# An encoder block on one core: the MLP's weight preparation as two streams, and earlier operands for its second product

## Chip, cores and metric

The kernel runs on one core of one Trainium2 chip. The metric is the device time of one execution in microseconds (us). Engines are named as the profile names them: PE (TensorE), DVE (VectorE), ACT (ScalarE), POOL (GpSimd) and SP, whose queue issues the DMAs.

## What is computed

A hybrid encoder block over 1024 tokens of 1024 channels, in float32. Only its last line matters here:

```
h = rms_norm(x, norm2_g) @ w_mlp_in            # 1024x1024 by 1024x4096
x = x + square(relu(h)) @ w_mlp_out            # 1024x4096 by 4096x1024
```

## The kernel before

**Precision.** Each float32 matrix is scaled by a power of two and split into two float16 parts, hi on ACT (a scaled copy) and lo on DVE (the scaled value less hi, one SCALAR_TENSOR_TENSOR). A product is three passes over these parts (PASSES, L473). The power of two comes from a bound on the matrix: ACT squares it and sums along each row, DVE adds the row sums (`sum_of`, L933) and copies the result to a bfloat16 column, PE sums over the 128 partitions with a matmul against ones (`all_sum`, L197; a 128x1 result, "ones" in the profile), and DVE makes the scale of it (`scale_of`, L940). `scale_of` holds the ones matmul back until PE has been given n whole units of work since the sum.

**Strassen's scheme in Winograd's form.** Both MLP products are done with seven half-size products instead of eight, so sums of quarters of each matrix are needed: for weights POOL makes them (`forms_sum`, L1067, four additions), for activations `sums` (L1274).

**First product.** The 4096 hidden channels are 16 groups (chunks) q of 128 + 128. A group is seven units (`seven`, L1126; `quad`, L1578), each 12 matmuls into one PSUM bank; the eight banks go round, so that a unit's bank is free again only when the unit eight places before it (sums over partitions counted) has been read. DVE combines each bank with earlier ones into `as`. Groups 0 and 1 are done in two halves of 256 tokens, 0, 1, 0, 1, because the last tokens' activations come late. When a group is done, `h_done` (L1551) gives its result relu and square on ACT, the four sums for the second product on POOL (for q of 0 and 1 on DVE), and stores it to HBM (`hs`).

**Weight preparation of a group** has two halves. `sums1(q)` (L1354): when the two raw tiles of weights are loaded, eight scalings in place on ACT (`rows_scaled`, L949), two squares with row sums on ACT (`squares`, L959), four sums on POOL, then `sum_of`. `prep1(q)` (L1369): `scale_of`, then, once group q - 3 is done on PE (`gate`, L1340) and its tile is free, the split `forms_split` (L1095) in four steps, each a hi part and a lo part (`parts`, L1081). After the second lo part two raw tiles count as free, and `load_upto` (L231) issues the loads of the next two; there are five raw tiles (`rawp`, L77). In the kernel before, one stream does split(q), then sums(q + 1), then split(q + 1) and so on.

**Second product.** 28 operand pairs, seven to each of four stages, are made by `prep2` (L1648), each an activation form and a weight form with hi and lo parts (`ops`), and taken by 4 units each (L1780). For stage 0 `first2` (L1730) issues the loads of w_2 (`w2x`) and of the first stored form.

**What orders the work.** Everything is emitted by one Python program; each engine gets its instructions in the order of emission, and waits for other engines through semaphores at its head. After each unit `unit` (L204) emits the unit's reading of its bank, delayed by one unit (`late`), then alternates `step` (advance every generator in `fg`: `h_done` and the like) and `tick` (advance the first generator of `bg`: preparation). A generator that yields WAIT lets the next one in `bg` run, if `side[0]` is set. In the first product a unit has 2 steps and 5 ticks (3 steps in groups 0 and 1's halves), in the second 2 and 4.

Of the kernel before, what the change touches and what calls it, by code (L numbers as in the profile page):

```python
# [10 lines left out]
F32 = mybir.dt.float32  # L11
F16 = mybir.dt.float16
# [58 lines left out]
def encoder_block(ctx: ExitStack, tc: tile.TileContext, x, weights, cols, gqk, rel, masks, out):  # L71
# [102 lines left out]
        forced[0] = False  # L174

    late, units, forced, side, splitting = [], [0], [False], [False], [False]
    work = [0]

    def apart(mark, n=3, of=units):
        while of[0] < mark + n and not forced[0]:  # L180
            yield WAIT
# [22 lines left out]
    def unit(mms, post=None, steps=0, ticks=0):  # L204

        for ps, l, r, a, b in mms:
            T.matmul(ps, l, r, start=a, stop=b)  # L207
        units[0] += 1
        work[0] += len(mms) * mms[0][0].shape[-1]
        settle()  # L210
        if post:
            late.append(post)
        for i in range(max(steps, ticks)):
            if i < steps:
                step()
            if i < ticks:
                tick()

    def settle():
# [861 lines left out]
    def parts(todo, s, then):  # L1081

        prev = None
        for n, it in enumerate(todo + [None]):
            if prev:
                o, w = prev
                V.scalar_tensor_tensor(o(1), w, sc[:, s], o(0), op0=OP.mult, op1=OP.subtract)
                then(n - 1)
            if it:
                o, w = it  # L1090
                A.activation(o(0), w, AF.Copy, scale=sc[:, s])
            prev = it
            yield
# [245 lines left out]

    def gate(i):  # L1340
        while pe_done[0] < i - 2:
            yield

    def need(i):
        while i not in ready:
# [23 lines left out]
    def prep1(q):  # L1369

        ch = c1[q]
        s, ch.inv = yield from scale_of(ch.sum, 9, 1)
        yield from gate(q)
        pool, tag = TAGS[q % 3]
        P = P1[q] = pool.tile([128, 7 if q else 8, 2, 512], F16, name="w16_1", tag=tag)
        yield from forms_split(ch, tsum[q], s, P)
        ready.add(q)
        if 1 < q < 15:
            yield from sums1(q + 1)

    SQJ = U2[1][:, 0, :, :, 384:512].rearrange("p s k t -> p (s k) t").bitcast(BF16)
    scaled = []
# [143 lines left out]
    def last_pair():  # L1526
        sq(7, 1)()
        normal(7, row3(7))
        yield from wait(3)
        form_sums()  # L1530
        high(3, 0), high(3, 1)
        yield from wait(6)
        low(3, 0)
        yield from wait(3)
        bg.append(sums1(2))
        bg.extend(prep1(q) for q in range(2, 16))
        yield from wait(6)
        low(3, 1)
        limit[0] = 10 ** 6
        load_upto(done[0] + 5)  # L1540
# [10 lines left out]
    def h_done(q, c0=0, c1=512, wait1=0, wait2=0):  # L1551

        f = AS[q] if c1 < 512 else AS.pop(q)
        v = f[:, :, c0:c1]
        yield from wait(wait1)
        A.activation(v[:, 0:4], v[:, 0:4], AF.Relu)
        yield
        A.activation(v[:, 0:4], v[:, 0:4], AF.Square, scale=sc[:, c1w[q].inv],
                     accum_out=sc[:, at(bsum[q // 4], 4 if c1 < 512 else q % 4)])
        yield  # L1560
        yield from wait(wait2)
        if q > 1:
            yield from sums(v, G)
        else:
            for _ in sums(v, V):
                pass
        if c1 < 512:
            return
        SP.dma_start(HS[q // 4][:, :, q % 4], f)
        live.remove(q)  # L1570
        if q % 4 == 3:
            m = tmp()
            V.tensor_reduce(sc[:, m], sc[:, bsum[q // 4]], axis=AX, op=OP.max)
            yield
            yield from pow2(m, 14, *R[q // 4])
            r_ready[q // 4] = True

    def quad(q, c0=0, c1=512):  # L1578
        need(q)
        if c0 == 0:  # L1580
            while q - 2 in live:
                step()
            live.add(q)
            AS[q] = w4p.tile([128, 7, 512], F32, name="as", tag="as")
        ps = {}
        z = [AS[q][:, i, c0:c1] for i in range(7)]
        if q == 2:
            z[4:6] = extra

        def post6(ps):  # L1590
            V.tensor_tensor(z[5], ps[6], z[4], op=OP.add)
            if c0:
                post5(ps)

        def post5(ps):
            V.tensor_tensor(z[1], ps[5], z[5], op=OP.subtract)

        def post7(ps):
            V.tensor_tensor(z[6], ps[7], z[5], op=OP.add)
            V.tensor_tensor(z[2], ps[4], z[6], op=OP.add)  # L1600
            V.tensor_tensor(z[3], ps[5], z[6], op=OP.subtract)

        def post3(ps):
            V.tensor_tensor(z[1], ps[3], z[1], op=OP.add)
            if q == 0:
                fg.append(h_done(q, c0, c1, 3, 4 if c0 else 24))
            elif c1 == 512:
                fg.append(h_done(q, 0, c1, *((2, 6) if q == 1 else ())))
        seven(P1[q], actU2, c0, c1, {
            1: lambda ps: A.activation(z[4], ps[1], AF.Copy),  # L1610
            6: post6, 5: None if c0 else post5,
            2: lambda ps: V.tensor_tensor(z[0], ps[2], z[4], op=OP.add),
            7: post7, 3: post3}, 2 if c1 == 512 else 3, 5, (1, 2, 5, 4, 6, 7, 3) if c0 else (1, 6, 5, 4, 2, 7, 3))

    def whole(q):
        quad(q)
        pe_done[0] = q + 1
# [7 lines left out]
    quad(1, 256, 512)  # L1625
    pe_done[0] = 2
    held[0] = 0
    for q in range(2, 14):
        whole(q)


    OPS, X2 = {}, {}
# [15 lines left out]
    def prep2(s):  # L1648
# [23 lines left out]
            G.tensor_tensor(T2[:, i], w12[i], w22[i], op=OP.add)  # L1672
            G.tensor_tensor(T2[:, i], T2[:, i], w11[i], op=OP.add)
        yield
        if s == 0:
            yield from gate(17)
            P = OPS[17] = TAGS[17 % 3][0].tile([128, 2, 2, 2048], F16, name="ops", tag=TAGS[17 % 3][1])
            later["h", 1] = P[:, 0].rearrange("p w m -> p (w m)").bitcast(F32).rearrange("p (k t) -> p k t", k=4)
            SP.dma_start(later["h", 1], HS[0][:, ORDER[1][0]])
        sw, inv = yield from scale_of(sums, 0)  # L1680
        fw = keep()
        mul(iR, sw, fw)
# [2 lines left out]
        for o, (f, name) in enumerate(ORDER):  # L1685
# [1 line left out]
            i = 16 + n  # L1687
            yield from gate(i)
            pool, tag = TAGS[i % 3]
            if n > 1:  # L1690
                OPS[i] = pool.tile([128, 2, 2, 2048], F16, name="ops", tag=tag)
            P = OPS[i]
            while ("h", n) not in later:
                yield
            if 1 < n < 25:
# [2 lines left out]
            A.activation(P[:, 1, 0], hf, AF.Copy, scale=sc[:, Rs])  # L1698
            yield
            V.scalar_tensor_tensor(P[:, 1, 1], hf, sc[:, Rs], P[:, 1, 0], op0=OP.mult, op1=OP.subtract)  # L1700
            w = {"w11": w11, "t1": w11, "t3": w12, "w21": w21, "w22": w22}.get(name) or [T2[:, i] for i in range(2)]
            for i2 in range(2):
                A.activation(P[:, 0, 0, 1024 * i2:1024 * i2 + 1024], w[i2], AF.Copy, scale=sc[:, fw])
            yield
            for i2 in range(2):
                sl = slice(1024 * i2, 1024 * i2 + 1024)
                V.scalar_tensor_tensor(P[:, 0, 1, sl], w[i2], sc[:, fw], P[:, 0, 0, sl], op0=OP.mult, op1=OP.subtract)
                yield
            ready.add(i)
            if name == "w11":  # L1710
# [24 lines left out]
        later["t2"] = lambda: h0[:, 1].rearrange("p (a k) t -> p a (k t)", a=2)  # L1735
        yield from wait(12)

    bg.append(first2())
    bg.append(prep2(0))
    whole(14)  # L1740
    whole(15)


    later["hf"] = base.tile([128, 4, 4, 512], F32, name="hf", tag="U")
# [129 lines left out]
```

## Time and profile before

| | us |
|---|---|
| three runs | 1237.73, 1239.75, 1241.18 |
| median | 1239.75 |
| the profiled execution's own time | 1236.77 |
| its span, first to last instruction | 1235.0 |
| mean granted clock of PE over the span | 0.994 |
| first product, groups 2 to 15, on PE | 680.5 to 938.2 |
| second product on PE | 938.2 to the end |

How to read it: spans and stage bounds are from one profiled execution. In timelines the columns are start, time until the last one ends, engine, line, operation, tile written and tiles read, shapes, count, and in brackets the idle time of the engine before it with what ended it. Most operations of DVE and ACT carry the line of a helper, L66, and are told apart by their tiles: `raw` are raw weights, `tsum` their sums, `w` the float16 parts, `as` the products of a group, `ops` operands of the second product, `hf`, `h` and `hs` the stored forms.

### The profile page before, as it was taken

Reading aid. Unit: us, or ns where it says so; the run is one execution under the profiler, and the core shown is the slowest. Engines: PE = TensorE matmul, PEld = TensorE weight load, DVE = VectorE, ACT = ScalarE, POOL = GpSimd, SP = SyncE. Lnnn points to the kernel's source line nnn. Section 1 sums busy time; section 2 is a strip of 40 time slices with the busy share of each in tenths; the row PEclk is TensorE's granted clock in tenths of the full one; section 3 lists DMA queues with packets and bytes.
Section 4 is the critical chain, followed back from the end, with each engine's and each line's share of the span. In section 5 each row is a group of like instructions: output and inputs, shape, how many; then the busy total and the mean of one; then the engine's idle time right before and its main releaser. Section 6 shows DMA issues by size and latency. Waiting matters only on the chain.

```text
span 1235.0 us, 16691 instructions
## 1 busy us (share of the span) xinstructions
PE 1196.9 (97%) x6102; PEld 576.9 (47%) x6102; DVE 936.9 (76%) x1747; ACT 765.9 (62%) x1185; POOL 430.3 (35%) x289
## 2 busy tenths in 40 slices
PE   5989999999899999999999999999999999999998
PEld 3534445555444444444458444444444444444444
DVE  6668778888558786877878664555547999999997
ACT  6777667768644454535768777777775763646430
POOL 2440003232212111101003466655648373463562
PEclk8999999999899999999999999999999999999999
DMA  6558455565761211216096653454474844435202
GB/s 258 107 200 178 103 118 112 116 153 105 131 154 34 69 52 51 69 35 255 18 174 152 205 170 137 162 187 142 140 290 162 313 155 159 168 116 222 103 35 103
DMA packets 170867, 173.34 MB, mean 140 GB/s; under 512 B 131488, under 2 KB 132000, under 8 KB 166688
## 3 DMA queue, kind: packets, MB, share of 16 engines
q1 hardware_dynamic: 170784, 172.27, 47.2%
q8 instruction: 48, 0.79, 0.3%
q14 instruction: 35, 0.29, 0.1%
HBM read 102.51 MB, written 37.75 MB: 114 GB/s over the span
## 4 chain that ended last, share of the span: by engine, by line
PE 40%; DVE 6%; ACT 2%; issue 2%; DMA 1%; DVEq 0%; ACTq 0%
PE ps_d L207 16%; PE ps_s L207 14%; PE ps_o L207 10%; DVE as L66 1%; DVE ops L66 1%; DVE w L66 1%; DVE form L66 1%; ACT as L66 1%; DVE v L66 1%; DMA u2T<-v 1%; DMA u2x<-v 1%; ACT ops L66 1%; DVE x L66 0%; DVE sc L66 0%; ACT u2x L66 0%
## 5 line engine op out<-in xcount | busy, mean ns | idle before, releaser
L207 PEld LDWEIGHTS <-ops 128*128 128x128 f16 x1356 | 132.4, 98 | 159.9 <-issue 2.7
L207 PEld LDWEIGHTS <-w 128*128 128x128 f16 x1368 | 132.8, 98 | 143.5 <-issue 3.8
L924 PE MATMUL ps_d<-uT,w_ws 128*128 128x512 f16 x576 | 136.7, 382 | 0.0
L207 PE MATMUL ps_s<-ops 128*128 128x512 f16 (+1 forms) x528 | 118.3, 374 | 0.0
L207 PE MATMUL ps_d<-ops 128*128 128x512 f16 x504 | 115.6, 379 | 0.0
L66 ACT ACTIVATE ops<-hf,sc 128x2048 f16<-128x2048 f32 x26 | 52.0, 1999 | 94.0 <-PE ps_d L207 52.7
L207 PE MATMUL ps_d<-u2T,w 128*128 128x512 f16 (+1 forms) x504 | 110.3, 371 | 0.0
L1074 POOL TENSOR_TENSOR tsum<-raw 128x512 f32<-128x512 f32 x28 | 46.6, 1677 | 148.1 <-ACT raw L66 148.1
L207 PEld LDWEIGHTS <-uT 128*128 128x128 f16 x648 | 64.9, 101 | 70.5 <-issue 5.6
L1278 POOL TENSOR_TENSOR as<-as 128x512 f32<-128x512 f32 x56 | 76.7, 1370 | 41.4 <-ACT as L66 38.1
L207 PEld LDWEIGHTS <-w_s 128*128 128x128 f16 x588 | 56.9, 98 | 68.6 <-DVE w_s L66 0.6
L924 PEld LDWEIGHTS <-w_ws 128*128 128x128 f16 x576 | 56.1, 98 | 59.7 <-issue 2.0
L207 PE MATMUL ps_s<-u2x,w 128*128 128x512 f16 (+1 forms) x348 | 78.6, 375 | 0.0
L207 PE MATMUL ps_o<-ops 128*128 128x512 f16 x324 | 74.3, 379 | 2.4 <-DVE as L66 2.4
L66 DVE SCALAR_TENSOR_TENSOR ops<-hf,sc,ops 128x2048 f16<-128x2048 f32 x26 | 71.7, 2759 | 5.7 <-ACT ops L66 5.7
L66 ACT ACTIVATE raw<-raw,sc 128x256 f32<-128x256 f32 x172 | 71.1, 494 | 6.7 <-DMA raw<-in_weights 6.7
L66 DVE TENSOR_TENSOR as<-ps_s,as 128x512 f32<-128x512 f32 (+1 forms) x38 | 23.4, 616 | 58.5 <-ACT as L66 57.9
L66 DVE TENSOR_SCALAR sc<-sc 128x1 int32<-128x1 int32 (+3 forms) x380 | 57.6, 167 | 12.9 <-ACT sq L66 4.3
L1074 POOL TENSOR_TENSOR gsum<-raw 128x512 f32<-128x512 f32 x14 | 18.5, 1340 | 136.8 <-issue 52.3
L66 ACT ACTIVATE w<-raw,sc 128x512 f16<-128x512 f32 (+1 forms) x29 | 25.4, 920 | 50.8 <-DVE sc L66 50.8
L66 ACT ACTIVATE sz<-sz,sc 128x384 f32<-128x384 f32 (+1 forms) x64 | 37.2, 581 | 26.8 <-DVE sc L66 26.6
L66 DVE SCALAR_TENSOR_TENSOR w_ws<-raw,sc,w_ws 128x512 f16<-128x512 f32 (+2 forms) x72 | 48.5, 712 | 6.7 <-ACT w_ws L66 6.7
(261 smaller groups left out, 2548.6 us busy)
## 6 DMA issues: line engine op xcount, KB each, us to landing
raw<-in_weights SPq DMA_DIRECT2D x89, 512.0 KB, 5.5
hs<-as SPq DMA_DIRECT2D x16, 1792.0 KB, 8.7
hf<-hs SPq DMA_DIRECT2D x26, 1024.0 KB, 6.7
w2x<-in_weights SPq DMA_DIRECT2D x16, 512.0 KB, 8.3
raw<-in_weights SPq DMA_DIRECT2D x16, 384.0 KB, 3.7
xt<-in_x SPq DMA_DIRECT2D x8, 512.0 KB, 9.8
gs<-s SPq DMA_DIRECT2D x4, 1024.0 KB, 6.4
x<-in_x SPq DMA_DIRECT2D x8, 512.0 KB, 10.0
```

The costliest lines, as they stand in the source:

```text
L66: return f(out, *a, **kw)
L207: T.matmul(ps, l, r, start=a, stop=b)
L924: T.matmul(ps, l, r, start=a, stop=b)
L1074: G.tensor_tensor(t[:, o], a, b, op=OP.add)
L1278: sub.tensor_tensor(z[o], z[a], z[b], op=op)
```

## The change

Weight preparation becomes two streams in `bg`, both started where the single one was. `all_sums` runs `sums1` for q = 2 to 15 and may be up to three chunks ahead of the split (it waits until q - 3 is ready). `all_preps` runs `prep1` for q = 2 to 15, each waiting until its chunk's sums are done, and then `first2` and `prep2(0)`. With `side[0]` set the splits run when the sums wait and the other way round. `scale_of` holds its ones matmul back by 2 units instead of 1 for q over 2. From group 2 to 15 `pace[0]` is 1: within one unit, ticks stop as soon as one lo part has been issued (`spent`). `first2` and `prep2(0)`, which stood before groups 14 and 15 in the program, now follow the last split; the second operand pair takes its tile and loads its form inside the loop, and then waits for 2 units' work. The four sums of group 1's result go to POOL and no longer wait 6 steps.

```diff
--- before.py
+++ after.py
@@ -174,7 +174,7 @@
         forced[0] = False
 
     late, units, forced, side, splitting = [], [0], [False], [False], [False]
-    work = [0]
+    work, spent, pace = [0], [0], [0]
 
     def apart(mark, n=3, of=units):
         while of[0] < mark + n and not forced[0]:
@@ -210,10 +210,11 @@
         settle()
         if post:
             late.append(post)
+        spent[0] = 0
         for i in range(max(steps, ticks)):
             if i < steps:
                 step()
-            if i < ticks:
+            if i < ticks and (not pace[0] or spent[0] < pace[0]):
                 tick()
 
     def settle():
@@ -1085,6 +1086,7 @@
             if prev:
                 o, w = prev
                 V.scalar_tensor_tensor(o(1), w, sc[:, s], o(0), op0=OP.mult, op1=OP.subtract)
+                spent[0] += 1
                 then(n - 1)
             if it:
                 o, w = it
@@ -1339,7 +1341,7 @@
 
     def gate(i):
         while pe_done[0] < i - 2:
-            yield
+            yield WAIT
 
     def need(i):
         while i not in ready:
@@ -1369,14 +1371,30 @@
     def prep1(q):
 
         ch = c1[q]
-        s, ch.inv = yield from scale_of(ch.sum, 9, 1)
+        while q > 1 and q not in summed:
+            yield WAIT
+        s, ch.inv = yield from scale_of(ch.sum, 9, 2 if q > 2 else 1)
         yield from gate(q)
         pool, tag = TAGS[q % 3]
         P = P1[q] = pool.tile([128, 7 if q else 8, 2, 512], F16, name="w16_1", tag=tag)
         yield from forms_split(ch, tsum[q], s, P)
         ready.add(q)
-        if 1 < q < 15:
-            yield from sums1(q + 1)
+
+    summed = set()
+
+    def all_sums():
+        for q in range(2, 16):
+            while q > 4 and q - 3 not in ready:
+                yield WAIT
+            yield from sums1(q)
+            summed.add(q)
+
+    def all_preps():
+        for q in range(2, 16):
+            yield from prep1(q)
+        side[0] = False
+        yield from first2()
+        yield from prep2(0)
 
     SQJ = U2[1][:, 0, :, :, 384:512].rearrange("p s k t -> p (s k) t").bitcast(BF16)
     scaled = []
@@ -1532,8 +1550,8 @@
         yield from wait(6)
         low(3, 0)
         yield from wait(3)
-        bg.append(sums1(2))
-        bg.extend(prep1(q) for q in range(2, 16))
+        side[0] = True
+        bg.extend([all_sums(), all_preps()])
         yield from wait(6)
         low(3, 1)
         limit[0] = 10 ** 6
@@ -1559,7 +1577,7 @@
                      accum_out=sc[:, at(bsum[q // 4], 4 if c1 < 512 else q % 4)])
         yield
         yield from wait(wait2)
-        if q > 1:
+        if q > 0:
             yield from sums(v, G)
         else:
             for _ in sums(v, V):
@@ -1605,7 +1623,7 @@
             if q == 0:
                 fg.append(h_done(q, c0, c1, 3, 4 if c0 else 24))
             elif c1 == 512:
-                fg.append(h_done(q, 0, c1, *((2, 6) if q == 1 else ())))
+                fg.append(h_done(q, 0, c1, *((2, 0) if q == 1 else ())))
         seven(P1[q], actU2, c0, c1, {
             1: lambda ps: A.activation(z[4], ps[1], AF.Copy),
             6: post6, 5: None if c0 else post5,
@@ -1625,8 +1643,6 @@
     quad(1, 256, 512)
     pe_done[0] = 2
     held[0] = 0
-    for q in range(2, 14):
-        whole(q)
 
 
     OPS, X2 = {}, {}
@@ -1672,11 +1688,6 @@
             G.tensor_tensor(T2[:, i], w12[i], w22[i], op=OP.add)
             G.tensor_tensor(T2[:, i], T2[:, i], w11[i], op=OP.add)
         yield
-        if s == 0:
-            yield from gate(17)
-            P = OPS[17] = TAGS[17 % 3][0].tile([128, 2, 2, 2048], F16, name="ops", tag=TAGS[17 % 3][1])
-            later["h", 1] = P[:, 0].rearrange("p w m -> p (w m)").bitcast(F32).rearrange("p (k t) -> p k t", k=4)
-            SP.dma_start(later["h", 1], HS[0][:, ORDER[1][0]])
         sw, inv = yield from scale_of(sums, 0)
         fw = keep()
         mul(iR, sw, fw)
@@ -1687,9 +1698,13 @@
             i = 16 + n
             yield from gate(i)
             pool, tag = TAGS[i % 3]
-            if n > 1:
+            if n:
                 OPS[i] = pool.tile([128, 2, 2, 2048], F16, name="ops", tag=tag)
             P = OPS[i]
+            if n == 1:
+                later["h", 1] = P[:, 0].rearrange("p w m -> p (w m)").bitcast(F32).rearrange("p (k t) -> p k t", k=4)
+                SP.dma_start(later["h", 1], HS[0][:, ORDER[1][0]])
+                yield from apart(work[0], 2 * 6144, work)
             while ("h", n) not in later:
                 yield
             if 1 < n < 25:
@@ -1698,6 +1713,7 @@
             A.activation(P[:, 1, 0], hf, AF.Copy, scale=sc[:, Rs])
             yield
             V.scalar_tensor_tensor(P[:, 1, 1], hf, sc[:, Rs], P[:, 1, 0], op0=OP.mult, op1=OP.subtract)
+            spent[0] += 1
             w = {"w11": w11, "t1": w11, "t3": w12, "w21": w21, "w22": w22}.get(name) or [T2[:, i] for i in range(2)]
             for i2 in range(2):
                 A.activation(P[:, 0, 0, 1024 * i2:1024 * i2 + 1024], w[i2], AF.Copy, scale=sc[:, fw])
@@ -1705,6 +1721,7 @@
             for i2 in range(2):
                 sl = slice(1024 * i2, 1024 * i2 + 1024)
                 V.scalar_tensor_tensor(P[:, 0, 1, sl], w[i2], sc[:, fw], P[:, 0, 0, sl], op0=OP.mult, op1=OP.subtract)
+                spent[0] += 1
                 yield
             ready.add(i)
             if name == "w11":
@@ -1735,10 +1752,10 @@
         later["t2"] = lambda: h0[:, 1].rearrange("p (a k) t -> p a (k t)", a=2)
         yield from wait(12)
 
-    bg.append(first2())
-    bg.append(prep2(0))
-    whole(14)
-    whole(15)
+    pace[0] = 1
+    for q in range(2, 16):
+        whole(q)
+    pace[0] = 0
 
 
     later["hf"] = base.tile([128, 4, 4, 512], F32, name="hf", tag="U")
```

## Prediction

> **What bounds the kernel now.** I read the page's first lines, then the stage's row in the table of windows, then who kept PE waiting from 680 us on.
>
> ```profile
> span 1235.0 us, 16691 instructions
> ...
> PE 1196.9 (97%) x6102; PEld 576.9 (47%) x6102; DVE 936.9 (76%) x1747; ACT 765.9 (62%) x1185; POOL 430.3 (35%) x289
> ```
>
> ```profile
> 680.00:902.00 222.00, 218.80 (x1028) 99.42 (x1026) 127.11 (x253) 163.65 (x241) 128.25 (x92) 1.00 0.50 166
> ```
>
> ```profile
> PE ps_o L207 <- DVE as L66: 4.8, 2, 2.4
> PE ps_s L198 <- DVE ones L66: 0.8, 1, 0.8
> ```
>
> PE is the bound. In the first MLP product it computes 218.80 of 222 us at granted clock 1.00; ACT works 163.65, DVE 127.11, POOL 128.25. From 680 us to the end PE waits 4.8 + 0.8 = 5.6 us in all. That is everything the change can win there, 0.45% of 1235.0; the rest can only be lost.
>
> The units around it, by their starts on PE:
>
> ```profile
> 671.34 1.47 PE L207 MATMUL ps_d<-u2T,w 128*128 128x256 f16 x12
> 672.65 1.47 PE L207 MATMUL ps_s<-u2T,raw 128*128 128x256 f16 x12
> ...
> 680.54 2.75 PE L207 MATMUL ps_d<-u2T,w 128*128 128x512 f16 x12
> ...
> 698.69 2.75 PE L207 MATMUL ps_d<-u2T,w 128*128 128x512 f16 x12
> ...
> 870.78 2.75 PE L207 MATMUL ps_o<-u2T,w 128*128 128x512 f16 x12
> ...
> 948.51 2.75 PE L207 MATMUL ps_o<-ops 128*128 128x512 f16 x12 [2.38 <-DVE as L66]
> ```
>
> A half unit takes 1.31 us (672.65 - 671.34), a whole one twice that, 2.59, so a group of seven whole units 18.15. Group 2 starts at 680.54, group 3 at 698.69. Group 3 holds the first 2.4 and the 0.8; the last unit of the first operand pair of the second product holds the other 2.4. The unit at 870.78 is the third of group 12.
>
> **The change, part by part.** Nothing is added to the arithmetic: the same lo parts, scalings and loads are issued in another order (only group 1's four sums go from DVE to POOL). So the cost is what now stands ahead of what. I went through the order in which each engine gets its instructions in the changed kernel and gave each the time of its row here.
>
> *Start-up, groups 0 and 1.* The sums of chunk 3 (eight scalings of raw weights and two squares on ACT) now stand ahead of the split of chunk 2; before, they stood behind it.
>
> ```profile
> 662.67 1.76 ACT L66 ACTIVATE w<-raw,sc 128x512 f16<-128x512 f32 x2 [1.32 <-DVE sc L66]
> ...
> 666.41 0.36 ACT L66 ACTIVATE as<-ps_s 128x256 f32<-128x256 f32 x1
> 667.94 3.30 ACT L66 ACTIVATE raw<-raw,sc 128x256 f32<-128x256 f32 x8 [1.17 <-DMA raw<-in_weights]
> 671.15 1.04 ACT L66 ACTIVATE tsum<-raw 128x1024 f32<-128x1024 f32 x1
> ...
> 673.37 0.36 ACT L66 ACTIVATE as<-ps_d 128x256 f32<-128x256 f32 x1
> ```
>
> ```profile
> 663.57 2.90 SPq L229 DMA_DIRECT2D raw<-in_weights  x4
> ```
>
> The raw weights land at 667.94 whatever ACT does: their load is issued only at 663.57, behind the transposes, and this the change leaves alone. So ACT now idles until 667.94, scales and squares until 673.4, and only then does the split (666.41 - 662.67 = 3.74 us), until 677.1, and the copy of a bank (0.36) until 677.5. On DVE, in order:
>
> ```profile
> 734.15 1.94 DVE L66 SCALAR_TENSOR_TENSOR w<-raw,sc,w 128x512 f16<-128x512 f32 x2
> 736.00 2.48 DVE L66 SCALAR_TENSOR_TENSOR w<-tsum,sc,w 128x1024 f16<-128x1024 f32 x2
> 738.39 0.68 DVE L66 TENSOR_TENSOR as<-ps_s,as 128x512 f32<-128x512 f32 x1
> ...
> 739.72 1.28 DVE L66 TENSOR_TENSOR as<-ps_o,as 128x512 f32<-128x512 f32 x2
> ...
> 746.51 0.16 DVE L66 CAST ones<-sc 128x1 bf16<-128x1 f32 x1
> ...
> 749.31 0.78 DVE L66 TENSOR_SCALAR sc<-sc 128x1 int32<-128x1 int32 x5
> ```
>
> Four lo parts trail the four hi parts; from the first hi (674.1) they take 1.85 + 2.4, to 678.5; then one combination (half width, 0.4) and a reduce and the cast (0.16 each and the gap) for the sum over partitions of the next chunk (0.35), to 679.3. That sum's matmul on PE stands right before the unit that started at 672.65 and waits for the cast: **6.7 us** of idle PE. Four in-place sums (half width, 1.8) and one combination later the second unit after it gets its bank, 0.8 late; and in group 2 the next sum's matmul waits likewise for chunk 3's split, which ACT ends at about 690.6 and DVE at 692.3, 1.6 after PE is there. Together 9.1 us: group 2 starts at 688.1, group 3 at 707.8.
>
> *The loop of groups 3 to 11.* Here lies the larger term. In each group the changed order on ACT is: relu, first hi part, square, second and third hi part, **four scalings of a raw tile whose load was issued only when this group's first lo part freed its buffer**, two squares, and then the fourth hi part. Behind that one's lo part stand on DVE all combinations of this group's last four units, and behind the last of them the next group's relu. That is a circle. "Sums ahead" is ahead of the split, but five raw tiles do not let the loads be ahead. Its prices, from a steady group of before:
>
> ```profile
> 777.38 1.89 ACT L66 ACTIVATE as<-as 128x2048 f32<-128x2048 f32 x1
> ...
> 779.30 2.00 ACT L66 ACTIVATE as<-as,sc 128x2048 f32<-128x2048 f32 x1
> ...
> 786.37 1.76 ACT L66 ACTIVATE w<-raw,sc 128x512 f16<-128x512 f32 x2 [4.49 <-DVE sc L66]
> 788.04 2.17 ACT L66 ACTIVATE w<-tsum,sc 128x1024 f16<-128x1024 f32 x2
> ```
>
> ```profile
> raw<-in_weights SPq DMA_DIRECT2D x6, 512.0 KB, 3.9
> ```
>
> ```profile
> hs<-as SPq DMA_DIRECT2D x8, 1792.0 KB, 8.7
> raw<-in_weights SPq DMA_DIRECT2D x14, 512.0 KB, 6.9
> ```
>
> ```profile
> L66 DVE SCALAR_TENSOR_TENSOR w<-tsum,sc,w x24: 1272/1279/2289, 700.0 to 900.6; 128x1024 f16<-128x1024 f32 x24
> ```
>
> Relu 1.92 (779.30 - 777.38), first hi 0.7, lo 0.75, load 4.0 (3.9 is the median from 450 to 500 us, where a raw load runs alone; 6.9 that from 740 to 880 us, where it is issued beside the 1792 KB store; in the new order the store is nearly through) = 7.4. ACT's own queue gets there at 1.92 + 0.6 + 2.0 + 1.07 + 0.5 + 1.04 = 7.1, so the load ends last. Scalings 1.6 (half of 3.2), squares 2.2, hi 1.1: 12.3. Lo part: 1.28 alone, 2.29 where POOL adds beside it. Then five combinations (two starts 1.33 apart, 0.67 each with the last's end: 3.3), reduce and cast 0.35, six small operations 1.0: 4.65. Sum: **18.25 or 19.25 us** against PE's 18.15. In the new order POOL starts this chunk's sums just before that lo part, as it does here at
>
> ```profile
> 699.98 4.49 DVE L66 SCALAR_TENSOR_TENSOR w<-tsum,sc,w 128x1024 f16<-128x1024 f32 x2
> ```
>
> ```profile
> 701.47 4.13 POOL L1074 TENSOR_TENSOR tsum<-tsum,raw 128x512 f32<-128x512 f32 x2 [0.28 <-ACT tsum L66]
> ```
>
> where two lo parts took 4.49, so I take 19.25; 18.25 stays as the lower end. The Trainium skill, "GPSIMD Engine Reference", section 1, Specifications, says that GpSimd's SBUF interfaces are shared with VectorE and that instructions with two SBUF inputs contend; by that rule, which speaks against this change, the lo part (two SBUF inputs) is slow in every group and the dear end holds. The row's minimum and median, 1272 and 1279, do not yet show it; its maximum does.
>
> The chain: group 2's ACT queue (scalings of two tiles loaded at 688 to 693, squares, copy, relu, square, hi parts, again two tiles scaled behind a load) brings the relu of group 3 to 716.3 or, with slow lo parts, 718.1. In group 3 four more scalings (1.6) and in group 3 and 4 the square (2.0) stand before the first hi, in group 4 also 0.7 of bound operations: loops of 21.8 and 21.0 (dear 22.8, 22.0). Relu of group 5: 759.1 or 762.9. Six loops more: 868.6 or 878.4, plus 14.25 or 15.25 to the first combination behind group 11's last lo part: 882.8 or 893.6. The third unit of group 12 reuses that combination's bank; it started at 870.78. So PE is late by 12.1 or **22.8 us**, the start-up's 9.1 and the old 3.2 of group 3 included. From group 12 on no load stands in the circle and DVE catches up.
>
> *The second product's operands.* Operands 16 and 17 are issued through groups 14 and 15, so the 2.38 before 948.51 goes: -2.4. What is late next: six squares stand in group 14 before the sum's cast, and its matmul comes after five units, not eight.
>
> ```profile
> 908.85 1.14 ACT L66 ACTIVATE ops<-raw,sc 128x1024 bf16<-128x1024 f32 x1
> ...
> 913.93 2.00 ACT L66 ACTIVATE ops<-w2x,sc 128x2048 bf16<-128x2048 f32 x1
> ...
> 917.97 0.18 ACT L66 ACTIVATION_READ_ACCUMULATOR ops<-w2x,sc 128x1 f32 x1
> ```
>
> Squares 918.2 - 908.85 = 9.3, relu, square and copy 4.4, combination and cast 1.1: 14.8 against 5 x 2.59 = 12.95, about +2.0. Loads of w_2 and the h tile move with them on SP behind the same stores; they are due ten or more us later and cost nothing unless the stores slip by that much. Group 1's sums on POOL free 2.9 us of DVE where DVE waits for ACT anyway: nothing.
>
> **Sum:** 22.8 - 2.4 + 2.0 = +22.4 on 1236.77, the profiled execution's own time (1235.0 of span and 1.8 around it): 1259.2. With the cheap lo part: +11.7, 1248.5. The three runs lie 1.0 to 4.4 above the profiled execution, their median 3.0; I don't add this, since it is less than the way back toward the cheap end. I forecast **1259**.
>
> **Rivals.**
> 1. *Faster:* the scalings never wait, because ACT reaches them after their load has landed, and DVE meets every bank. Then the 5.6 us go: 1231.2. It decides if the load of chunk 3's tiles lands before ACT is free, at 661.35 (662.67 less the 1.32 of idle in that row), and the loops stay under 18.15. For it: 0.1 to 1.1 us part the loop from PE's period. Against it: ACT's row at 667.94, which waits for that very load.
> 2. *Start-up only:* the loop is hidden, being under 18.15, and the 9.1 stay: 9.1 - 3.2 - 2.4 + 2.0 = +5.5, 1242.3; with the runs' offset up to 1246.
> 3. *Longer loads:* the 1792 KB store, 8.7 us in the row above, slips into the raw load, 6.9 instead of 3.9: eight loops by 3.0, +24 more, 1283. Against it: the store is issued behind POOL's four sums, near the middle of the circle, and should be through about when the next group's first load starts.
> 4. *Clock:* the new idle times lower PE's clock.
>
> ```profile
> 322.00:325.70 3.70, 0.84 (x4) 0.20 (x2) 2.89 (x15) 3.70 (x10) 0.79 (x1) 1.00 0.57 107
> 325.70:329.20 3.50, 3.41 (x28) 2.19 (x29) 1.01 (x3) 3.47 (x8) 1.82 (x3) 0.51 1.24 152
> 329.20:332.60 3.40, 1.19 (x6) 0.34 (x4) 0.31 (x2) 0.92 (x2) 1.33 (x3) 1.00 0.74 120
> 332.60:336.00 3.40, 3.12 (x22) 1.91 (x23) 0.64 (x1) 0.60 (x1) 1.08 (x1) 0.50 0.51 114
> ```
>
> In two stretches of 3.7 and 3.4 us PE worked only 0.84 and 1.19; in the 3.4 us behind each the clock stood at 0.51 and 0.50, which costs 1.7 of work. The gaps of 6.7 in group 1 and of some 4 in groups 4 and 5 may each do so: at most +5, 1264, at least nothing, for PE is then waiting for DVE's circle anyway. "TensorE: Matmul & The Clock Gate" of the Trainium skill, Part 1, gives half clock after an idle window of about 3.4 us and full clock after a busy one; by that rule the 6.7 us cost such a window.
>
> That the pacing is without effect is no case: each unit issues one lo part.
>
> **How the numbers follow.** Circle with one of the two lo prices, 1248 to 1262: 0.60. Longer loads or clock, 1262 and up: 0.18. Start-up only: 0.12. Faster: 0.06; the rest, near no change, 0.04. Range 1246 to 1273. About 0.3% (3.7 us) is what a measurement of this kernel can tell from no change: faster 0.06, within it 0.05, slower 0.89.
>
> **What would show it.** PE idle of 6 to 7 us before a 128x1 matmul near 672, released by DVE; ACT idle ahead of its raw scalings for a load, in each of groups 3 to 11; group starts there 18.3 to 19.3 us apart instead of 18.15; no idle before the fourth unit of the second product. Wrong if the first wait is missing, or if groups 5 to 12 stay at 18.15 apart.

## The result and the profile after

The changed kernel takes **1255.49 us** (median of four runs, 1254.55 to 1256.59) against 1239.47 (four runs): 1.013 of before, 95% interval 1.0112 to 1.0147, 16.0 us slower. The profiled execution has 1253.2 of span, 18.2 more than before's (whose profiled execution, 1236.77, lies below its four runs). First the page's line on the engines, then PE's longest waits from 640 us on:

```profile
PE 1201.0 (96%) x6102; PEld 577.8 (46%) x6102; DVE 942.6 (75%) x1743; ACT 765.7 (61%) x1185; POOL 452.5 (36%) x293
```

```profile
PE ps_s L198 <- DVE ones L66: 9.5, 2, 8.9
PE ps_d L198 <- DVE ones L66: 4.0, 1, 4.0
PE ps_d L207 <- DVE as L66: 3.6, 2, 3.3
PE ps_d L207 <- DVE sc L66: 2.7, 2, 2.4
```

No work was added, but PE is busy 4.1 longer (1201.0 against 1196.9), and from 640 us on it waits 20.2 where before it waited 6.3. The places, on PE's timeline:

```profile
682.04 0.19 PE L198 MATMUL ps_s<-ones 128*128 128x1 bf16 x1 [8.86 <-DVE ones L66]
682.09 2.72 PE L207 MATMUL ps_o<-u2T,raw 128*128 128x256 f16 x12
...
691.61 2.75 PE L207 MATMUL ps_d<-u2T,w 128*128 128x512 f16 x12
695.05 0.16 PE L198 MATMUL ps_s<-ones 128*128 128x1 bf16 x1 [0.68 <-DVE ones L66]
...
710.64 2.75 PE L207 MATMUL ps_s<-u2T,w 128*128 128x512 f16 x12
...
737.44 2.75 PE L207 MATMUL ps_d<-u2T,w 128*128 128x512 f16 x12 [3.30 <-DVE as L66]
...
758.17 2.75 PE L207 MATMUL ps_d<-u2T,w 128*128 128x512 f16 x12 [2.42 <-DVE sc L66]
...
831.21 2.75 PE L207 MATMUL ps_d<-u2T,w 128*128 128x512 f16 x12 [0.26 <-DVE sc L66]
...
885.67 2.75 PE L207 MATMUL ps_d<-u2T,w 128*128 128x512 f16 x12
...
933.90 0.16 PE L198 MATMUL ps_d<-ones 128*128 128x1 bf16 x1 [4.02 <-DVE ones L66]
933.93 4.43 PE L207 MATMUL ps_s<-u2x,w 128*128 128x512 f16 x12
```

Group 2 starts at 691.61 (before 680.54), group 3 at 710.64 (698.69), the third unit of group 12 at 885.67 (870.78). Subtracting gives the table; "half clock" is a unit that took 2.72 instead of 1.47, or 4.43 instead of 2.75, where the table of windows shows PE's granted clock (third number from the end) at 0.52 and 0.60; behind the gap of 3.30 it stayed at 1.00:

```profile
680.00:685.00 5.00, 2.77 (x13) 1.82 (x14) 4.86 (x10) 3.74 (x9) 1.52 (x2) 0.52 0.31 105
...
737.40:740.20 2.80, 2.76 (x13) 1.27 (x13) 2.66 (x9) 0.00 (x0) 0.51 (x1) 1.00 0.00 0
...
933.90:938.20 4.30, 4.29 (x14) 1.59 (x14) 2.62 (x9) 1.87 (x1) 4.22 (x3) 0.60 0.00 0
```

| stage | forecast | measured |
|---|---|---|
| start of group 2 | +7.6 | +11.1 |
| start of group 3 | +9.1 | +12.0 |
| third unit of group 12 | +22.8 (cheap end +12.1) | +14.9 |
| sum over partitions in group 14, with half clock behind it | +2.0 | +4.0 + 1.7 |
| stall before the second product's fourth unit | -2.4 | -2.4 |
| end | +22.4 | +18.2 |

Why the first wait, on ACT and DVE:

```profile
669.10 3.52 ACT L66 ACTIVATE raw<-raw,sc 128x256 f32<-128x256 f32 x8 [7.34 <-DMA raw<-in_weights]
...
674.75 1.74 ACT L66 ACTIVATE w<-raw,sc 128x512 f16<-128x512 f32 x2
...
675.49 3.52 DVE L66 SCALAR_TENSOR_TENSOR w<-raw,sc,w 128x512 f16<-128x512 f32 x2 [12.06 <-ACT w L66]
...
681.83 0.16 DVE L66 CAST ones<-sc 128x1 bf16<-128x1 f32 x1
```

ACT stands idle for 7.34 us at the head of chunk 3's scalings, with chunk 2's split, ready to go, queued behind them. The forecast's order is there to the instruction; each of its times is one to three us later (ACT's scalings 669.10 against 667.94, the end of the cast 682.0 against 679.3).

A steady group (the relu of one group to that of the next), from the timelines of ACT, DVE and SP put together:

```profile
834.71 1.91 ACT L66 ACTIVATE as<-as 128x2048 f32<-128x2048 f32 x1 [5.20 <-DVE as L66]
...
838.04 3.95 SPq L230 DMA_DIRECT2D raw<-in_weights  x2
...
841.68 1.69 ACT L66 ACTIVATE raw<-raw,sc 128x256 f32<-128x256 f32 x4
...
845.50 1.13 ACT L66 ACTIVATE w<-tsum,sc 128x1024 f16<-128x1024 f32 x1
...
846.66 2.00 DVE L66 SCALAR_TENSOR_TENSOR w<-tsum,sc,w 128x1024 f16<-128x1024 f32 x1 [2.19 <-ACT w L66]
...
852.82 1.91 ACT L66 ACTIVATE as<-as 128x2048 f32<-128x2048 f32 x1 [4.59 <-DVE as L66]
```

```profile
L66 DVE SCALAR_TENSOR_TENSOR w<-tsum,sc,w x23: 1412/1692/2002, 715.1 to 914.7; 128x1024 f16<-128x1024 f32 x23
```

The last row has all low (lo) parts made from `tsum`, the third and fourth of each group, in groups 3 to 13, but for group 3's third (2.29, at 708.53), which starts ahead of the window (least, median, longest in ns). The same row of before, from the same window (715 to 916 us):

```profile
L66 DVE SCALAR_TENSOR_TENSOR w<-tsum,sc,w x22: 1272/1279/1281, 718.1 to 900.6; 128x1024 f16<-128x1024 f32 x22
```

One turn takes 852.82 - 834.71 = **18.11** us, PE's seven units 18.15. The turn is the forecast's: relu, split, load, scalings, last high part, low part beside POOL (2.00), combinations, next relu. ACT does not wait for the load here (no bracket at 841.68): from 700 us on its scalings did so in three groups only (at 710.10, 730.37 and 750.08).

### The profile page after: what moved, and what is told of

The parts are those of the page before. It is cut to its first block, busy times and chain, and to the rows that moved or that the text cites. A ratio compares the mean times of both kernels' runs of the same rounds, so it can differ in the third digit from the quotient of the medians.

```text
span 1253.2 us, 16709 instructions
## 1 busy us (share of the span) xinstructions
PE 1201.0 (96%) x6102; PEld 577.8 (46%) x6102; DVE 942.6 (75%) x1743; ACT 765.7 (61%) x1185; POOL 452.5 (36%) x293
## 5 line engine op out<-in xcount | busy, mean ns | idle before, releaser
L207 PEld LDWEIGHTS <-w 128*128 128x128 f16 x1368 | 133.1, 98 | 152.7 <-issue 14.3
L1280 POOL TENSOR_TENSOR as<-as 128x512 f32<-128x512 f32 x60 | 104.0, 1733 | 92.9 <-ACT as L66 89.5
L207 PE MATMUL ps_d<-u2T,w 128*128 128x512 f16 (+1 forms) x384 | 84.3, 369 | 6.0 <-DVE as L66 3.3
L66 DVE SCALAR_TENSOR_TENSOR w<-raw,sc,w 128x512 f16<-128x512 f32 (+1 forms) x29 | 34.1, 1182 | 72.4 <-ACT w L66 72.4
L66 ACT ACTIVATE raw<-raw,sc 128x256 f32<-128x256 f32 x172 | 72.2, 495 | 21.6 <-DMA raw<-in_weights 21.5
L207 PE MATMUL ps_s<-u2T,w 128*128 128x512 f16 (+1 forms) x360 | 76.2, 361 | 0.2 <-DMA u2T<-v 0.2
L66 ACT ACTIVATE as<-as 128x2048 f32<-128x2048 f32 (+1 forms) x17 | 30.7, 1808 | 65.9 <-DVE as L66 65.9
L207 PE MATMUL ps_o<-u2x,w 128*128 128x512 f16 (+1 forms) x312 | 69.0, 371 | 0.0
L66 DVE SCALAR_TENSOR_TENSOR w<-tsum,sc,w 128x1024 f16<-128x1024 f32 x28 | 47.6, 1706 | 26.9 <-ACT w L66 26.9
```

The lines of the kernel that those rows point to most:

```text
L66: return f(out, *a, **kw)
L1280: sub.tensor_tensor(z[o], z[a], z[b], op=op)
```

## The experiments

The theory: the sums' place ahead of the split costs the start-up, and a circle as long as PE's group carries the loss to the end. The rivals: the waits are of single places, found again or not; the pacing makes them; the circle has room.

**1. Chunk 3's sums behind chunk 2's split** (in the changed kernel).

```diff
-            while q > 4 and q - 3 not in ready:
+            while q == 3 and 2 not in ready or q > 4 and q - 3 not in ready:
```

> The changed kernel, but chunk 3's sums are issued only once chunk 2 is split. Theory (what stands ahead of the split on ACT and DVE makes the first wait, and PE loses it for good): the 8.86 us before the 128x1 matmul at 682, the slow unit behind it (2.72 instead of 1.47) and the 0.26 and 0.68 in group 2 go, together 11.1; the old 3.2 of group 3 or something like it comes back: 1246 to 1248, from 1255.5. Rival (the circle relu, split, load, scalings, split, combinations sets the time of group 12 whatever PE does before it): the first wait goes, but the 3.3 and 2.4 in groups 4 and 5 grow by as much, to 14 or more together: 1253 to 1256.

1284.76, ratio to before 1.0354 (1.0334 to 1.0373): neither. The first wait went, as both expected, but the edit also turned round two DMAs on SP's queue in groups 3 to 8. SP, then ACT:

```profile
752.62 0.53 SPq L1587 DMA_DIRECT2D hs<-as  x1
753.23 1.73 SPq L230 DMA_DIRECT2D raw<-in_weights  x2
```

```profile
762.13 1.70 ACT L66 ACTIVATE raw<-raw,sc 128x256 f32<-128x256 f32 x4 [11.58 <-DMA raw<-in_weights]
```

The load stands behind the store of 1792 KB, which waits for POOL's sums; it lands 8.9 us after its issue, and ACT idles 11.58 with the fourth high part behind it; PE waits up to 10.3 in one group. That is the mechanism of the forecast's rival "longer loads"; the changed kernel escapes it, because its load is issued first (746.59, the store 752.15). So this run is no test of the start-up alone.

**2. The ones matmul of group 14 three units later** (in the changed kernel).

```diff
-        sw, inv = yield from scale_of(sums, 0)
+        sw, inv = yield from scale_of(sums, 0, 6 if s == 0 else 3)
```

> The changed kernel, but the matmul that sums over the partitions for the second product's scale comes three units later. Theory (the 4.02 us in group 14 is only a matmul placed ahead of its six squares, and the slow unit behind it, 4.43 instead of 2.75, is the clock after that gap): 4.0 + 1.7 = 5.7 less, 1249.8; operands 16 and 17 still in time, no wait before the first unit on ops. Rival (the operands' scale is what is late, so the wait moves to the first unit on ops): at most 2 less, 1253.5 or more.

1262.72, 1.018 (1.0163 to 1.0196), 6 to 7 more than the changed kernel. The rival's mechanism, at a higher price: the 4.02 went, and PE waits for operands:

```profile
956.21 2.53 PE L207 MATMUL ps_o<-ops 128*128 128x512 f16 x11 [1.79 <-DVE ops L66]
970.61 0.58 PE L207 MATMUL ps_d<-ops 128*128 128x512 f16 x1 [4.10 <-ACT ops L66]
972.98 2.72 PE L207 MATMUL ps_d<-ops 128*128 128x512 f16 x6 [1.78 <-DVE ops L66]
```

So the sum in group 14 can't simply come later: the operands that need its scale are then late. A part of the 7 is a unit at half clock in group 4 (5.28 instead of 2.75), behind a gap of 3.42.

**3. One square more for each of chunks 6 to 13** (in the changed kernel).

```diff
+            if ch in c1[6:14]:
+                A.activation(t[:, 2:4].rearrange("p a c -> p (a c)"), ch.raw[1], AF.Square, accum_out=sc[:, tmp()])
```

> The changed kernel with one further square (1.04 us and its 0.19 readout) behind the two of each of chunks 6 to 13, into a column that nobody reads. Theory (the circle of one group takes 18.1 us, as much as PE's seven units, so it has no slack): each of the eight groups 4 to 11 becomes 1.2 longer, +9.6: 1265. Rival (the circle is shorter by over 1.2 and only follows PE in groups 6 to 11): just groups 4 and 5, where PE waits already, get longer: +2.4, 1258.

1265.69, 1.0204 (1.0181 to 1.0227): the theory's 1265. PE's third units of three groups in a row:

```profile
763.79 2.75 PE L207 MATMUL ps_d<-u2T,w 128*128 128x512 f16 x12 [0.81 <-DVE sc L66]
...
783.13 2.75 PE L207 MATMUL ps_d<-u2T,w 128*128 128x512 f16 x12 [1.02 <-DVE sc L66]
...
802.46 2.75 PE L207 MATMUL ps_d<-u2T,w 128*128 128x512 f16 x12 [1.01 <-DVE sc L66]
```

They are 19.34 and 19.33 apart, 18.11 + 1.23: what one adds on ACT comes out at PE in full. So the circle has no slack in these groups, though in the changed kernel PE hardly waits there (0.26 in group 9).

**4. One square less** (the second square of chunks 6 to 13 left out, so that the scale comes from half the weights).

```diff
+            if i and ch in c1[6:14]:
+                return at(sm, 0)
             A.activation(junk, ch.raw[i], AF.Square, accum_out=sc[:, at(sm, i)])
```

> The changed kernel with the second of the two squares of chunks 6 to 13 left out, so that their scale comes from half of the weights. Theory (the circle sets the waits of groups 4 and 5, and from group 6 on PE's own 18.15 holds): only the 3.30, 2.42 and 0.26 can shrink, by 1.2 in each group with a square less: -2.4 to -3, 1252.5 to 1253. Rival (the circle is what ends last in every group): 1.2 in each of eight groups, up to -6, where these waits are used up: 1249.5. If the waits are the start-up's alone and no circle is behind them: no change.

1250.41, 1.0079 (1.0062 to 1.0096), 5 to 6 less. The waits of groups 4, 5 and 9 shrank as the theory said, from 3.30, 2.42 and 0.26 to 1.80, 1.18 and none, 3.0 together. The rest is in group 14: 4.02 became 1.55, with no half clock behind it. These places add up to 7.2; the profiled span is only 3.4 shorter, since this execution was late already before the first wait, and one more half unit behind it ran at half clock. In the changed kernel a circle without slack had kept DVE behind PE up to group 14, which neither theory had priced.

**5. Chunk 3's first load between the last two transposes** (in the changed kernel).

```diff
         low(3, 0)
+        limit[0] = 10 ** 6
+        load_upto(done[0] + 5)
         yield from wait(3)
...
         low(3, 1)
-        limit[0] = 10 ** 6
-        load_upto(done[0] + 5)
```

> The changed kernel, with the first two raw tiles that the transposes hold up loaded between the last two transposes (about 660) instead of behind both (664.35), so that they land near 664.6. Theory (the first wait of 8.86 is ACT's 7.34 of waiting for that load, handed on through the split of chunk 2, and is not found again later): ACT waits some 3, the first wait falls to about 4.4, the slow unit behind it stays or goes (1.3), and the last transpose is late by up to 3, of which PE has 3 to 4 in hand: 4 to 6 less, 1249.5 to 1251.5. Rival (the loads that land at 680 to 694 hold the circle of groups 3 to 5 back whatever the first wait is): the gain comes back in groups 4 and 5, 1254 or more.

1253.43, 1.012 (1.0103 to 1.0138), an interval that overlaps the changed kernel's: by the time alone, inconclusive. The trace tells more. The load landed at 664.75, and the 8.86 became 2.35 (for the late transpose, with half clock behind it: 2.47 instead of 1.47) and 1.57; but group 4 took more:

```profile
670.82 2.47 PE L207 MATMUL ps_d<-u2x,w 128*128 128x256 f16 x12 [2.35 <-DMA u2x<-v]
...
734.09 5.28 PE L207 MATMUL ps_d<-u2T,w 128*128 128x512 f16 x12 [3.56 <-DVE as L66]
```

Group 2 started 4.1 earlier (687.54 instead of 691.61), but at the third unit of group 9 only 1.8 of that was left (829.38 instead of 831.21): the unit at half clock took 2.5 more, and there were new waits of 0.90 and 0.41 in groups 8 and 9, for the 2.42 of group 5 that went. At the end nothing was left (1253.0 of span). That the load makes the first wait is shown; that the start-up's loss reaches the end undiminished is not.

**6. The second product's part alone on the kernel before** (without the pace; operand 17's tile and `h` load as in the change).

```diff
-        if s == 0:
-            yield from gate(17)
...
+            if n == 1:
...
+    bg.append(second())
+    for q in range(2, 16):
+        whole(q)
```

> The kernel before with only the second product's part: operand 17 is allocated and its h tile loaded in its turn, and the two steps are issued through groups 14 and 15 behind the last split. Theory (the 2.4 before the fourth unit goes; the sum over the partitions comes two units earlier than in before, while the single stream's ACT is not late there): PE waits 0 to 2 before that sum, -2.4 to -0.4 from 1239.5 to 1240.6: 1237 to 1240. Rival (this part alone makes the 4.0 and the slow unit of 1.7 in group 14): +3.3, 1243. Second rival (operands 16 and 17 get late, as when the sum came three units later in the changed kernel): +5 or more.

1244.91, 1.0048 (1.0031 to 1.0065). The 2.38 went, and 0.97 before the earlier sum, then 2.52 and 1.22 in the third operand came instead: ACT waited 7.09 for that operand's `hf` load. A unit there ran at half clock (1.4 more), and two later sums waited 1.15 and 0.60. So this part costs 6 by itself: the price of the second rival, but in the third operand and not in operands 16 and 17.

**7. The pacing alone on the kernel before**, and **8. the changed kernel without it.**

```diff
+    pace[0] = 1
     for q in range(2, 14):
         whole(q)
+    pace[0] = 0
```

> The kernel before with only the pacing of groups 2 to 13: after a unit no further step of the stream once a low part has been issued. Theory (the loss comes from the order of two streams, not from the pace): within 3 of before, 1237 to 1243, with the 2.4 of group 3 perhaps gone and each later sum one to three units later on PE. Rival (spreading the low parts makes the combinations or the next split late): PE waits in most groups, 1248 or more.

> The changed kernel without the pacing: both streams may go on after a low part. Theory (order of the streams makes the loss): the first wait stays at 8 to 9, the waits of groups 4 and 5 change by less than 3, the rest stays: 1252 to 1258. Rival (the pacing holds the fourth high part back, and that makes the circle long): no waits in groups 4 and 5, 1249 or less.

1278.21, 1.0316 (1.0297 to 1.0334), and 1270.32, 1.0255 (1.0237 to 1.0273). In 7 the theory fell and its rival held; in 8 theory and rival both fell. With the pacing alone the split of each group is late for the group itself, and PE waits for the low part in the middle of a unit in every group from 771 us on:

```profile
775.85 2.33 PE L207 MATMUL ps_d<-u2x,w 128*128 128x512 f16 x10 [1.83 <-DVE w L66]
...
797.37 2.33 PE L207 MATMUL ps_d<-u2x,w 128*128 128x512 f16 x10 [1.84 <-DVE w L66]
```

That is 21.5 a group, and PE waits another 13.5 for operands of the second product. Without the pacing, seven combinations instead of five stand behind the fourth low part on DVE, and the circle is longer than PE's group (19.3 to 21.7 from one fourth low part to the next, from 793 us on). So the two halves of the change need each other: all but the pacing +32, the pacing (of groups 2 to 13) alone +39, together +16.

**9. and 10. Pacing in group 3 alone, and in groups 2 and 3 alone** (on the kernel before; `pace[0] = 1 if q == 3 else 0`, or `q < 4`).

> The kernel before with the pacing in group 3 alone, so that the combinations of group 3 stand between its low parts and not behind all four. Theory (the 2.4 and 0.8 that PE waits in group 3 are the two low parts of 4.49 us ahead of the combinations, a stall of one place; pacing is harmful only where it goes on, because each group then loses some lead): both waits go and nothing is late later, 2.4 to 3.2 less: 0.9974 to 0.998 of before. Rival (the split of group 4's chunk, issued two to three units later, never catches up): PE waits for low parts from some later group on, as with the pacing in all groups, 1243 or more.

> The kernel before with the pacing in groups 2 and 3 alone. Theory: as with group 3 alone, the two waits of 3.2 go, and the unpaced stream keeps the lead that is left: 1235 to 1238. Rival (three units of lead lost are one too many): PE waits for low parts in the later groups, 1245 or more. That tells how much of the lead is needed.

1258.9, 1.0151 (1.0128 to 1.0173), and 1241.17, 1.0012 (1.0001 to 1.0024). With group 3 alone the theory fell; the rival has the size, but not the place: the 2.41 stayed, PE waits 0.6 to 1.8 for the sum in eight later groups, and the stall in the second product grew from 2.38 to 6.40. With both, PE does not wait at all from 664 to 943 us, but the stall in the second product is 5.69, with half clock behind it. Why two paced groups do better than one stays open.

**11. Group 1's four sums on POOL, alone on the kernel before.**

```diff
-        if q > 1:
+        if q > 0:
             yield from sums(v, G)
...
-                fg.append(h_done(q, 0, c1, *((2, 6) if q == 1 else ())))
+                fg.append(h_done(q, 0, c1, *((2, 0) if q == 1 else ())))
```

> The kernel before with only the third small part of the change: group 1's four sums on POOL instead of DVE, and no six further steps ahead of them. Theory (DVE waits for ACT there anyway, and POOL has room): no change, 0.999 to 1.001 of before. Rival (POOL's sums, 1.28 us each, push its sums of the next chunk's weights, and with them the low parts of groups 2 and 3, later): 1 to 3 more, in group 3's waits of 2.4 and 0.8.

**1235.75**, 0.9968 (0.9954 to 0.9982): faster, which neither expected. DVE in group 3, first of before, then of this kernel (whose times are 2.36 later at the same place):

```profile
694.32 2.86 DVE L66 TENSOR_TENSOR as<-as 128x512 f32<-128x512 f32 x4
697.10 2.96 DVE L66 SCALAR_TENSOR_TENSOR w<-raw,sc,w 128x512 f16<-128x512 f32 x2
...
704.39 0.68 DVE L66 TENSOR_TENSOR as<-ps_s,t 128x512 f32<-128x512 f32 x1
```

```profile
696.67 2.95 DVE L66 SCALAR_TENSOR_TENSOR w<-raw,sc,w 128x512 f16<-128x512 f32 x2
699.55 3.49 DVE L66 SCALAR_TENSOR_TENSOR w<-tsum,sc,w 128x1024 f16<-128x1024 f32 x2
702.96 0.68 DVE L66 TENSOR_TENSOR as<-ps_s,t 128x512 f32<-128x512 f32 x1
```

The four sums (2.86) stood right ahead of the low parts whose combinations PE waits for. Without them the low parts start 2.8 sooner and the last two take 3.49 instead of 4.49, the combinations come 3.8 sooner, and both waits of group 3, 2.41 and 0.79, are gone. The edit also drops six steps of waiting; the two parts were not tried one by one.

**12. The same with pacing in groups 14 and 15 alone.**

```diff
+    pace[0] = 1
     whole(14)
     whole(15)
+    pace[0] = 0
```

> The kernel before with group 1's four sums on POOL (which alone gave 0.9968 of before) and with the pacing in groups 14 and 15 alone, where operands 16 and 17 are split. Theory (the 2.4 before the second product's fourth unit is two low parts of 5.31 us ahead of the last combinations on DVE, and pacing puts the combinations between them): that wait goes too, 0.9968 less 0.002, 0.995 of before or 1233. Rival (the pacing there only moves the last low parts of operand 17 behind their own first unit, so that PE waits for ops): 0.997 or more.

**1232.27** against 1240.21, 0.9932 (0.9917 to 0.9948): faster than both kernels. DVE before, then here, and PE here:

```profile
940.63 5.31 DVE L66 SCALAR_TENSOR_TENSOR ops<-h,sc,ops 128x1024 f16<-128x1024 f32 x2 [1.28 <-ACT ops L66]
945.86 0.68 DVE L66 TENSOR_TENSOR as<-ps_s,as 128x512 f32<-128x512 f32 x1
...
947.78 0.68 DVE L66 TENSOR_TENSOR as<-ps_o,as 128x512 f32<-128x512 f32 x1
```

```profile
937.24 1.40 DVE L66 TENSOR_TENSOR as<-ps_d,as 128x512 f32<-128x512 f32 x2
938.56 0.68 DVE L66 TENSOR_TENSOR as<-ps_o,as 128x512 f32<-128x512 f32 x1
939.16 1.47 DVE L66 SCALAR_TENSOR_TENSOR ops<-h,sc,ops 128x1024 f16<-128x1024 f32 x1
```

```profile
941.33 2.75 PE L207 MATMUL ps_s<-ops 128*128 128x512 f16 x12
943.92 2.75 PE L207 MATMUL ps_o<-ops 128*128 128x512 f16 x12
```

Four of the five combinations now stand ahead of operand 17's weight low parts, and the fourth unit follows the third without a gap. The 5.6 us that the forecast named as all there was to win from 680 us on are gone from the trace, by the change's smallest part and its pacing kept to two groups, without its two streams. The interval, 6.4 to 10.3 us, is a little more than 5.6. Where the rest is from wasn't traced; half clock behind the two stalls, which the profiled execution of before doesn't have, is one candidate. Of before's 47 runs beside these experiments, 19 had a mean clock of 0.990 to 0.992 and took 1239.4 to 1244.2, 28 had 0.993 or 0.994, as the profiled one, and took 1235.9 to 1240.6.

## Why the prediction was right, and where its steps failed

**The bound and the sign** held: no work was added, and of the 18.2 us PE's waits are 13.9 (20.2 - 6.3) and half clock behind two of them 2.9; the rest was not traced.

**Start-up:** right in kind, 9.1 forecast, 12.0 measured. The three waits were 8.86, 0.26 and 0.68 (9.8), forecast 6.7, 0.8 and 1.6 (9.1). ACT's load landed 1.2 later (669.10 instead of 667.94), the first two low parts took 3.52 instead of 1.94, beside POOL's sums of chunk 3 (674.98 to 677.92), and the gap cost half clock in one half unit (1.25).

**The loop** was the mis-sized term: "so I take 19.25" measured 18.11. The low part was near its dear end (2.00, forecast 2.29), and slow in every group (minimum 1412 ns in the row above, maximum 1281 in before's row of the same window). That agrees with the rule cited from "GPSIMD Engine Reference" of the Trainium skill; but here order decides whether it costs DVE anything (last section). ACT, however, reached its scalings 6.97 after the relu, not 7.4, since the load landed before ACT was there (3.5 median instead of 4.0), and the combinations took 4.2 instead of 4.65; scalings, squares and last high part were as forecast. One square more or less (3 and 4) shows that the circle is real and has no slack; it is just no longer than PE's group. So the first two loops paid: 21.35 and 21.04 from relu to relu (719.28, 740.63, 761.67), where the forecast had 21.8 and 21.0 cheap, 22.8 and 22.0 dear, and PE waited 3.30 and 2.42. The six behind them took 18.21 each (to 870.91), forecast 18.25 or 19.25, and PE waited 0.26. That is +14.9, near the cheap end. The step that failed is the loop's dear sum: its low part came nearly at the dear price, but its load and its combinations below theirs.

**From group 12 on "DVE catches up"** was right in part: the turns there take 16.0 and 14.5, but in group 14 the relu still starts 2.79 behind the group (919.56 against 916.77). In experiment 4, where DVE has caught up, it starts 0.93 behind it. The forecast counted relu, squares and cast from the group's start. So 1.9 of the 2.8 is DVE's lag, and 0.9 is a term missing from the sum; the work itself took 14.3, forecast 14.8.

**"Group 1's sums on POOL: nothing"** failed too: in the kernel before this part of the change is worth 3.7 us (experiment 11). DVE did not wait for ACT at that place; the sums were ahead of what PE waited for. How much they save inside the changed kernel wasn't tried.

**The rivals.** "Faster" fell with the first wait, and "start-up only" with the 3.30 and 2.42 of the circle, though it was not far off in groups 6 to 11. "Longer loads" did not happen here but in experiment 1. The clock cost 1.25 + 1.68 = 2.9, inside its bound of 5, on top of the main case and not in place of it; of the gaps it named the one in group 1 brought half clock, those in groups 4 and 5 did not, and the one in group 14, which it did not name, did.

**The signs.** The first wait came (8.86), and the one before the second product's fourth unit went. ACT waited for a load in three groups and not in each of 3 to 11. PE's third units are 20.73 apart from group 4 to 5 and 18.58 from 8 to 9, but 18.15 or 18.16 in the other six steps up to group 12. So by the forecast's own test ("if groups 5 to 12 stay at 18.15 apart") its loop failed from group 6 on, save in group 9.

The sum came out near because errors cancelled: groups 3 to 12 were given 13.7 (22.8 - 9.1) and took 2.9 (14.9 - 12.0), 10.8 too much; the start-up was 2.9 and group 14 3.7 too short. Together 4.2 too much, 22.4 against 18.2. That the time was met so closely is luck: with the loop as measured and the forecast's other terms the sum is 9.1 + 2.9 - 2.4 + 2.0 = 11.6, or 1248.4.

## What to carry to other kernels

When an operation is moved ahead of another on an in-order engine, ask first for what it waits: here its load, not its 7 us of work, made the stall, and the ready split stood behind it. A stall of a few us at one place is better mended at that place: find what stands directly ahead of the late instruction on its queue, and move that (0.9932), before the whole order is changed (1.013). A circle through several engines that is as long as the bound engine's period shows no waits in the trace and still has no room: lengthen it by a known amount to see.

## What the runs showed of the hardware

- **Whether a gap brings half clock hangs on where it lies, not on its length alone.** In the changed kernel the units behind gaps of 2.42 and 3.30 took 2.75, those behind 4.02 and 8.86 were slow (4.43; 2.72 for a half unit); gaps of 3.42 and 3.56 (experiments 2 and 5) were followed by 5.28. But in experiment 1 a gap of 2.33 was followed by 4.34, and in experiment 9 one of 2.41 by 4.44, where before has 2.75 behind 2.41. The clock records explain it. In them half clock comes in whole stretches of 3.41 us (up to four in a row) on a grid that runs through (in the changed kernel from 677.94 and from 933.94, 75 stretches apart). A gap counts by what it takes of one stretch: the 2.41 of experiment 9 lies whole in one, and the next is at half clock; an edge of the grid divides that of before:

```profile
706.22:709.64 3.42, 1.01 (x6) 0.39 (x4) 3.38 (x5) 0.00 (x0) 2.38 (x2) 1.00 1.01 289
709.64:713.05 3.41, 3.41 (x9) 1.18 (x8) 0.44 (x1) 2.91 (x2) 0.00 (x0) 0.50 0.60 233
```

  In before the stretches 701.21 to 704.63 and 704.63 to 708.04 have PE busy for 2.82 and 1.59. In all 14 traces (50 to 1220 us), each of the 49 stretches at full clock in which PE was idle for 2.1 us or more was followed by one at half clock, and none with less than 1.95; in between there were both. The Trainium skill, "TensorE: Matmul & The Clock Gate", Part 1, gives half clock after an idle window of about 3.4 us and calls the window free-running. These rows agree with the window's length and that it doesn't start with the gap; but a window idle for some 60% was enough, and there the measurement decides.
- **A raw load of 512 KB** lands in 3.5 (median of 740 to 880 us) when it is issued ahead of the 1792 KB store, and took 8.9 behind it.
- **A low part waits for the addition that POOL has begun, not for one that begins later.** All 23 low parts in the changed kernel's row (the steady group above) start while an addition of POOL is under way; each ends 1.08 or 1.09 us behind that addition and so takes 1.41 to 2.00 (at 846.66 there are 0.92 left of it: 2.00). Of before's 22, ten also overlap an addition, but they start 0.15 to 0.34 ahead of it and take 1.27 or 1.28 like the others (at 846.13, POOL from 846.35); there POOL's first addition is the one that gets longer (2.2 instead of 1.28).
